# Encoder trunk on one Trainium2 core: output-projection operands, early gate/up units and GpSimd's share in attention

## The chip, the cores and the metric

The kernel runs on one core of a Trainium2 chip. The metric is the device time of one execution in microseconds (us). The core has five instruction streams that matter here: TensorE (PE in the profile, with PEld for the loading of weights), VectorE (DVE), ScalarE (ACT), GpSimd (POOL) and SyncE (SP), which only issues transfers. SP and POOL each have a queue of transfers; an instruction that waits holds up whatever stands behind it on its engine.

## The reference

Two layers over 512 tokens of 1024 channels, 16 heads of 64. Layer 0 mixes tokens by 2-D neighbourhood attention over an 8 x 64 grid, layer 1 by three dilated sliding windows with a distance penalty. Every layer is

```python
h = rms_norm(x, norm_mix_pre[layer])
h = neighbourhood_attention(h, ...) if layer % 2 == 0 else dilated_attention(h, ...)   # each ends in  o @ w_o
x = x + rms_norm(h, norm_mix_post[layer])
h = rms_norm(x, norm_ffn_pre[layer])
x = x + rms_norm(swiglu(h, w_gate, w_up, w_down), norm_ffn_post[layer])
```

with `swiglu(x) = (silu(x @ w_gate) * (x @ w_up)) @ w_down`. In layer 1 the scores of a window get `- slope[head] * distance` before the softmax, and -1e30 outside the window.

## The kernel before

**Arithmetic.** Every large product is made in three matmuls (`mm3`, L375 to L379): each operand is split into a high and a low part (`split`, L363: a copy with rounding on ScalarE, L364, a subtraction on VectorE, L365), and high x high, high x low and low x high are added in a PSUM bank. The query/key, value, gate/up and down products are also arranged as seven products of half-size blocks in place of eight. For gate/up and query/key a class `Seven` (L404) holds one *unit*, a pair of 128-column weight blocks over 512 tokens. Its first step, `first` (`p1` and `p2`), splits the raw weights and makes two products of 12 matmuls each, from the operands X1A and X1B (token tiles 0 and 1). The other steps need sums of weight blocks (`sums`, L441 to L451, adds on GpSimd and VectorE) and operands that also hold token tiles 2 and 3 (D1, S2, S4, S3, X2B). `run` (L551) orders the steps of a unit among those of the following ones.

**Stages.** Norm and transposes; values and then, head pair by head pair (j = 0 to 7), query/key unit and attention; output projection; gate/up, 22 units; down; then the same for layer 1.

**Neighbourhood attention** (L1115 to L1140): for each head, scores, `softmax` numerators in four blocks (`window_softmax`), one reciprocal for the row sums (L1132), a scaling of the four blocks by it on GpSimd (L1134), transposes, products with the values. `keep` (L1027) copies the result of a head pair out of PSUM, split in high and low, and sends it to DRAM (`rvd`) from GpSimd's queue; in layer 0 the copy puts the elements in another order, and it is the writing that is strided (L1139). The pair 7 stays on the chip.

**Dilated attention** (L1237 to L1271): the bias of a head is `SLOPES[head] * dist`, made on GpSimd (`bias`, L1239) from a table of distances in `memc`, in one buffer of 768 columns for both heads; `softmax_pair` subtracts it on VectorE (L1234).

**Output projection** (`mix_out`, L1036, and `out_proj`, L771): `rvd` is loaded back into `rxa`. Eight weight units k, 128 rows each, are split: four into the ring of split weights `wslot` (four buffers, L369, shared with the query/key and gate/up units), one into `rxa`, three into `rxb`. `product(t)` adds the eight k of one token tile in two banks, in the order of k. For each token tile follow the norm after the mixer (`post`), the norm before gate/up (`pre`) and the operands of gate/up (`ops`): `postnorm_sum` (L642), `prenorm` (L589, L591), additions on GpSimd (L622 to L628), transposes (L598) and their copies (L600, L601).

**Gate/up** (`gate_up`, L818): three units are begun before the loop over the 22; `sink` evacuates into `memc` (L834, L835). Raw weights lie in two buffers of a pool and in three of an arena that takes the place of `rxb`. `down` follows; its norm gain is loaded by `gain` (L573), from GpSimd's queue like the others.

**Memory.** `arena` (L332) stacks buffers on a left and a right side. In layer 0, attention's `ao0` and `akl` lie on the right; `memc` takes their place.

**Order.** The program's order is not the order of execution. `Order` (L130) takes all instructions, the dependences between them (also those through buffers of a ring, arenas that lie over one another, and banks) and a table of costs (`_cost`, L77), runs a list schedule forward and backward several times, and pins every engine's stream, SP's and POOL's too, to the order of the best run (`pin`, L279). So an edit of a few lines can move instructions anywhere.

Of the kernel before, what the change touches and what calls it, by code (L numbers as in the profile page):

```python
# [295 lines left out]
def encoder_kernel(ctx: ExitStack, tc: tile.TileContext, a: dict, out: bass.AP):  # L296
# [29 lines left out]
    mem = cpool.tile([P, MEM], F32, name="mem")  # L326
    rvd = [dpool.tile([PAIRS, P, D], F32R, name=f"rvd{i}") for i in range(2)]

# [243 lines left out]

    def gain(g, row, queue=nc.gpsimd):  # L573
        queue.dma_start(g, bass.AP(tensor=row.tensor, offset=row.offset, ap=[[0, P], [1, D]]))  # L574
        return g
# [242 lines left out]
    def gate_up(layer, xs, hid, more, rings, sums):  # L818
# [29 lines left out]

        ahead = 3
        for f in range(ahead):  # L850
            unit_of(f).first()
        for f in range(FT):
            for i in range(f, min(f + 2, FT)):
                if i not in us:
                    us[i], units[i].p5 = next(u_), next(p5_)
            run(unit_of(f), unit_of(f + 1), unit_of(f + ahead))
            if sums and f % 2 == 0:
                sums.pop(0)(units[f].added)
# [151 lines left out]
    def hl(mem, i, n):  # L1010
        return mem[:, i * D:i * D + n], mem[:, i * D + n:i * D + 2 * n]
# [15 lines left out]
    def keep(layer, j, o, ost_, view):  # L1027

        mem = next(ost_) if j < PAIRS - 1 else rxa[:, j * D:(j + 1) * D]
        h, l = (view(v) for v in hl(mem, 0, 512))  # L1030
        act.activation(h, o, AF.Copy)
        dve.tensor_sub(l, o, h.bitcast(F32))
        if j < PAIRS - 1:
            nc.gpsimd.dma_start(rvd[layer][j], mem)

    def mix_out(layer, w, rxb, load_x):  # L1036
        for j in range(PAIRS - 1):
            nc.gpsimd.dma_start(rxa[:, j * D:(j + 1) * D], rvd[layer][j])
        us = [None] * 4 + [hl(rxa, 8, D)] + [hl(rxb, 2 * i, D) for i in range(3)]

        out_proj(w, rv, layer, load_x, us, (ring(mem, 4 * D, D, 4), ring(mem, 0, D, 4), ring(mem, 13440, 512, 2)),
                 (mem[:, 11392:11392 + D], mem[:, 12416:12416 + D]))

    def ffn(layer, stack):
        hl_ = ring(rxc, 0, D, 5)
# [4 lines left out]
        with arena(f"raw{layer}", 6 * D) as more:  # L1050
            gate_up(layer, xs, hid, more, (ring(memc, 0, 512, 4), ring(memc, 2 * D, 512, 2), ring(mem, MEM - 512, 256, 2)),
                    sums[layer])
# [62 lines left out]
    for j in range(PAIRS):  # L1115
# [8 lines left out]
        for hd in range(2):  # L1124
            h = 2 * j + hd
            bt = next(bias_)
            nc.sync.dma_start(bt, a["na_bias"][h])
            mn, sm, rc = (small(f"{n}0_{h}", 4) for n in ("mn", "sm", "rc"))
            pr = (next(p_), next(p_))

            views = window_softmax(q, kd, kl, hd, bt, pr, mn, sm, f"0_{h}")
            dve.reciprocal(rc, sm)  # L1132
            for i in range(4):
                pool.tensor_scalar(views[i], views[i], rc[:, i:i + 1], 1.0, op0=ALU.mult, op1=ALU.mult)  # L1134
            pts.append(window_transposed(next(pt_), views, f"0_{h}"))
        o = bank("o", f"o0_{j}")
        window_pv(o, vq[j // 2], pts, j)

        keep(0, j, o.rearrange("p (c i) -> p c i", i=ROWS), ost_,  # L1139
             lambda v: v.rearrange("p (i c) -> p c i", i=ROWS))  # L1140

    inner.close()
    memc = ctx.enter_context(arena("memc", 3 * D, "right"))
    mix_out(0, a["na_o"], rxb, lambda xt, t: nc.sync.dma_start(xt, a["x_rows"][t]))
    stack.close()
    rxb = ffn(0, stack)


# [6 lines left out]
    pt_, few_ = ring(ap, 10 * D, D, 4), ring(mem, 0, 96, 2)  # L1155
    bt, dist, qs, ks = memc[:, 0:768], memc[:, 768:1536], memc[:, 1536:2048], memc[:, 2048:2560]
    p5_ = ring(memc, 2560, 256, 2)
    q_, k_, kl_, ost_ = rxc[:, 0:D], rxc[:, D:2 * D], rxc[:, 2 * D:3 * D], ring(rxc, 3 * D, D, 1)
    w22_ = w22_ring(rxc[:, 4 * D:5 * D])
    b6 = bt.rearrange("p (k c) -> p k c", c=P)  # L1160

    b2h = b6[:, 4:6], b6[:, 0:2]
    nc.gpsimd.dma_start(dist, a["dist"])

    def by_token(v):
# [70 lines left out]

    def bias(j, hd, c, o=None):  # L1237
        o = bt[:, c] if o is None else o
        pool.tensor_scalar(o, dist[:, c], SLOPES[2 * j + hd], 1.0, op0=ALU.mult, op1=ALU.mult)  # L1239

    def scores_a(j, hd, b2):
        if b2 == 0:
            bias(j, hd, slice(0, 4 * P))
        s, pr = bank("s", f"sa_{j}_{hd}_{b2}"), next(p_)
        for b in (2 * b2, 2 * b2 + 1):
# [6 lines left out]
            i0 = i if b % 2 == 0 else after(i, i0)  # L1252
        softmax_pair(pr, s, ((b6[:, 1:3], b6[:, 0:2]), (b6[:, 0:2], b6[:, 0:4:3]))[b2], stats[j][0], hd, b2)
        parts[0, j, hd, b2] = pr

    def scores_b(j, c2):

        if c2 == 0:
            bias(j, 0, slice(4 * P, 6 * P))
            bias(j, 1, slice(4 * P, 6 * P), bt[:, 0:2 * P])  # L1260
        ss = [bank("s", f"sb_{j}_{hd}_{c2}") for hd in range(2)]
# [253 lines left out]
```

## Time and profile before

| | |
|---|---|
| median of 3 runs | 1505.38 us (1505.06 to 1508.24) |
| profiled execution, own time | 1505.72 us |
| its span, first to last instruction | 1503.9 us |
| mean granted TensorE clock | 0.992 |
| DMA moved | 247.25 MB |

A line of the profile names an engine, a line of the kernel, an operation, `out<-in` by the names of buffers, and a duration; `[1.62 <-DVE ao L1032]` is idle time before an instruction and what ended it. A line "A:B" is a window in us from the start of the span. Matmuls overlap, so a busy TensorE counts each from its start to its modelled end. "PEclk" is the share of its full clock that TensorE was granted.

### The profile page before, as it was taken

Reading aid. Unit: us, or ns where it says so; the run is one execution under the profiler, and the core shown is the slowest. Engines: PE = TensorE matmul, PEld = TensorE weight load, DVE = VectorE, ACT = ScalarE, POOL = GpSimd, SP = SyncE. Lnnn points to the kernel's source line nnn. Section 1 sums busy time; section 2 is a strip of 40 time slices with the busy share of each in tenths; the row PEclk is TensorE's granted clock in tenths of the full one; section 3 lists DMA queues with packets and bytes.
Section 4 is the critical chain, followed back from the end, with each engine's and each line's share of the span. In section 5 each row is a group of like instructions: output and inputs, shape, how many; then the busy total and the mean of one; then the engine's idle time right before and its main releaser. Section 6 shows DMA issues by size and latency. Waiting matters only on the chain.

```text
span 1503.9 us, 27938 instructions
## 1 busy us (share of the span) xinstructions
PE 1450.8 (96%) x10788; PEld 1335.8 (89%) x10788; DVE 1206.0 (80%) x1884; ACT 895.1 (60%) x1787; POOL 604.8 (40%) x484
## 2 busy tenths in 40 slices
PE   7999999999999999999999999999998999999997
PEld 7988877899999888999999998888977999999885
DVE  5499976898998878788678667887748989898876
ACT  4477754555555657554467766877764645555664
POOL 5357754534331002676455554445316423330001
PEclk9999999999999999999999999999999999999999
DMA  5347483856474674455344875672664232234662
GB/s 197 134 177 173 159 288 139 244 155 194 154 190 146 188 227 160 138 156 189 119 141 161 191 210 162 191 167 89 218 205 168 85 113 101 97 105 148 202 206 88
DMA packets 82117, 247.25 MB, mean 164 GB/s; under 512 B 18816, under 2 KB 29056, under 8 KB 79936
## 3 DMA queue, kind: packets, MB, share of 16 engines
q1 hardware_dynamic: 70064, 180.32, 36.5%
q0 software_dynamic: 11776, 64.88, 16.3%
q8 instruction: 85, 1.39, 0.4%
q14 instruction: 48, 0.39, 0.1%
q10 hardware_dynamic: 144, 0.26, 0.0%
HBM read 223.31 MB, written 68.26 MB: 194 GB/s over the span
## 4 chain that ended last, share of the span: by engine, by line
PE 78%; DVE 9%; DMA 5%; ACT 4%; issue 2%; POOL 1%; SPq 0%; POOLq 0%; DVEq 0%; ACTq 0%
PE gu L376 9%; PE gu L377 9%; PE gu L378 9%; PE pp_d L376 4%; PE pp_d L378 4%; PE pp_d L377 4%; PE yd_s L376 3%; PE yd_s L377 3%; PE yd_s L378 3%; PE vd L376 2%; PE vd L377 2%; PE yd_pp L376 2%; PE vd L378 2%; PE yd_pp L377 2%; PE yd_pp L378 2%
## 5 line engine op out<-in xcount | busy, mean ns | idle before, releaser
L377 PE MATMUL gu<-rxa,h_b 128*128 128x256 f32 x352 | 99.4, 283 | 3.6 <-DVE rxa L601 3.6
L376 PE MATMUL gu<-rxc,h_a 128*128 128x256 f32 x352 | 100.0, 286 | 2.3 <-ACT rxc L600 2.3
L376 PE MATMUL gu<-rxa,h_b 128*128 128x256 f32 x352 | 98.9, 282 | 2.3 <-ACT rxa L600 2.3
L376 PE MATMUL gu<-rxa,h_c 128*128 128x256 f32 x352 | 99.9, 284 | 0.6 <-DVE memc L838 0.5
L377 PE MATMUL gu<-rxc,h_a 128*128 128x256 f32 x352 | 100.3, 285 | 0.0
L378 PE MATMUL gu<-rxc,l_a 128*128 128x256 f32 x352 | 100.2, 285 | 0.0
L378 PE MATMUL gu<-rxa,l_b 128*128 128x256 f32 x352 | 99.0, 282 | 0.0
L377 PE MATMUL gu<-rxa,h_c 128*128 128x256 f32 x352 | 98.5, 280 | 0.0
L378 PE MATMUL gu<-rxa,l_c 128*128 128x256 f32 x352 | 98.3, 280 | 0.0
L364 ACT ACTIVATE rxc<-mem 128x512 fp32r<-128x512 f32 (+2 forms) x90 | 55.8, 624 | 65.6 <-PE yd_pp L377 34.6
L444 POOL TENSOR_TENSOR raw<-raw 128x512 f32<-128x512 f32 x24 | 36.4, 1516 | 123.6 <-DVE l_a L365 109.4
L365 DVE TENSOR_TENSOR rxc<-mem,rxc 128x512 fp32r<-128x512 f32 (+2 forms) x90 | 65.6, 733 | 20.5 <-ACT rxc L364 18.7
L444 POOL TENSOR_TENSOR r_gu<-r_gu 128x512 f32<-128x512 f32 x20 | 29.9, 1495 | 109.1 <-DVE l_a L365 105.5
L444 POOL TENSOR_TENSOR r_d<-r_d 128x512 f32<-128x512 f32 x24 | 37.1, 1546 | 88.4 <-DVE l_ad L365 53.2
L377 PEld LDWEIGHTS gu<-rxa,h_b 128*128 128x128 f32 x352 | 67.0, 190 | 4.0 <-DVE rxa L601 4.0
L376 PEld LDWEIGHTS gu<-rxc,h_a 128*128 128x128 f32 x352 | 68.0, 194 | 2.8 <-ACT rxc L600 2.8
L1235 ACT ACTIVATE mem<-mem 128x256 f32<-128x256 f32 x128 | 63.6, 501 | 10.1 <-DVE mem L1234 9.8
L376 PEld LDWEIGHTS gu<-rxa,h_b 128*128 128x128 f32 x352 | 67.1, 191 | 2.7 <-ACT rxa L600 2.7
L376 PEld LDWEIGHTS gu<-rxa,h_c 128*128 128x128 f32 x352 | 66.3, 188 | 2.4 <-DVE memc L838 1.3
L377 PEld LDWEIGHTS gu<-rxc,h_a 128*128 128x128 f32 x352 | 68.0, 193 | 0.0
L378 PEld LDWEIGHTS gu<-rxc,l_a 128*128 128x128 f32 x352 | 67.6, 192 | 0.0
L574 POOL DMA_DIRECT2D mem<-g_ffn_post x2 | 1.2, 612 | 164.0 <-DVE rxc L365 164.0
(603 smaller groups left out, 6242.8 us busy)
## 6 DMA issues: line engine op xcount, KB each, us to landing
wsum<-wd POOLq DMA_DIRECT2D x24, 1408.0 KB, 11.4
r_d<-dil_qk SPq DMA_DIRECT2D x48, 512.0 KB, 4.8
raw<-wg SPq DMA_DIRECT2D x24, 512.0 KB, 3.7
raw<-wu SPq DMA_DIRECT2D x24, 512.0 KB, 4.7
wsum<-wsum POOLq DMA_DIRECT2D x8, 1408.0 KB, 8.0
raw<-wsum SPq DMA_DIRECT2D x22, 512.0 KB, 4.3
r_gu<-wg SPq DMA_DIRECT2D x20, 512.0 KB, 3.8
r_gu<-wu SPq DMA_DIRECT2D x20, 512.0 KB, 4.6
```

The lines of the kernel that those rows point to most:

```text
L364: act.activation(h, src, AF.Copy)
L365: dve.tensor_sub(l, src, h.bitcast(F32))
L376: i = pe.matmul(o, s[0], m[0], start=start, stop=False, skip_group_check=True)
L377: pe.matmul(o, s[0], m[1], start=False, stop=False, skip_group_check=True)
L378: pe.matmul(o, s[1], m[0], start=False, stop=stop, skip_group_check=True)
L444: self.added = e[0].tensor_add(q[0], q[0], q[2])
L574: queue.dma_start(g, bass.AP(tensor=row.tensor, offset=row.offset, ap=[[0, P], [1, D]]))
L1235: act.activation(pr[:, f], pr[:, f], AF.Exp, bias=st[:, c:c + 1], scale=-1.0, accum_out=st[:, c + 2:c + 3])
```

## The change

- `rvd` is an F32 buffer, and `keep` stores to it from SP's queue; loading it back stays with GpSimd's. `gain` uses SP's queue by default.
- Layer 0: the scalings of blocks 1 and 3 of each head go to ScalarE; blocks 0 and 2 stay on GpSimd. `keep` gets a view of the PSUM bank in the order of the output, so that its reading is strided and its writing contiguous.
- Layer 1: the bias of every head is computed on the host (`dil_bias`, 6 x 128 columns a head) and loaded in two pieces a head (four and two blocks) from SP's queue, into a buffer of 1536 columns, where each head and each kind of window has a place of its own. The table of distances and its load go.
- Output projection: units 2 and 3 are split into a new arena `wm` (3 x 1024 columns, the last half of unit 3 in `vmem`), not into the ring; the ring holds only units 0 and 1. `wm` is open only during the output projection; `memc` is opened anew after it, in each layer, in the same place.
- Gate/up: five units are begun before the loop, and the loop begins the sixth when it comes to f = 2. The ring of gate buffers has five, for that; the second buffer for `up` moves to `mem`.

```diff
-    rvd = [dpool.tile([PAIRS, P, D], F32R, name=f"rvd{i}") for i in range(2)]
+    rvd = [dpool.tile([PAIRS, P, D], F32, name=f"rvd{i}") for i in range(2)]
...
-    def gain(g, row, queue=nc.gpsimd):
+    def gain(g, row, queue=nc.sync):
...
-        ahead = 3
-        for f in range(ahead):
+        ahead, early = 3, 5
+        for f in range(early):
             unit_of(f).first()
...
-            run(unit_of(f), unit_of(f + 1), unit_of(f + ahead))
+            run(unit_of(f), unit_of(f + 1), unit_of(f + ahead) if f + ahead >= early else None)
...
-            nc.gpsimd.dma_start(rvd[layer][j], mem)
+            nc.sync.dma_start(rvd[layer][j], mem.bitcast(F32))
...
-    def mix_out(layer, w, rxb, load_x):
+    def mix_out(layer, w, rxb, wm, load_x):
...
-        us = [None] * 4 + [hl(rxa, 8, D)] + [hl(rxb, 2 * i, D) for i in range(3)]
+        us = [None] * 2 + [hl(wm, 0, D), (wm[:, 2 * D:], vmem), hl(rxa, 8, D)] + [hl(rxb, 2 * i, D) for i in range(3)]
...
-            gate_up(layer, xs, hid, more, (ring(memc, 0, 512, 4), ring(memc, 2 * D, 512, 2), ring(mem, MEM - 512, 256, 2)),
+            gate_up(layer, xs, hid, more, (ring(memc, 0, 512, 5), cycle([memc[:, 2560:3072], mem[:, 13520:14032]]), ring(mem, MEM - 512, 256, 2)),
...
-                pool.tensor_scalar(views[i], views[i], rc[:, i:i + 1], 1.0, op0=ALU.mult, op1=ALU.mult)
+                if i % 2:
+                    act.activation(views[i], views[i], AF.Copy, scale=rc[:, i:i + 1])
+                else:
+                    pool.tensor_scalar(views[i], views[i], rc[:, i:i + 1], 1.0, op0=ALU.mult, op1=ALU.mult)
...
-        keep(0, j, o.rearrange("p (c i) -> p c i", i=ROWS), ost_,
-             lambda v: v.rearrange("p (i c) -> p c i", i=ROWS))
+        keep(0, j, o.rearrange("p (c i) -> p i c", i=ROWS), ost_,
+             lambda v: v.rearrange("p (i c) -> p i c", i=ROWS))
...
-    memc = ctx.enter_context(arena("memc", 3 * D, "right"))
-    mix_out(0, a["na_o"], rxb, lambda xt, t: nc.sync.dma_start(xt, a["x_rows"][t]))
+    with arena("wm0", 3 * D, "right", F32R) as wm:
+        mix_out(0, a["na_o"], rxb, wm, lambda xt, t: nc.sync.dma_start(xt, a["x_rows"][t]))
     stack.close()
-    rxb = ffn(0, stack)
+    memc = inner.enter_context(arena("memc0", 3 * D, "right"))
+    rxb = ffn(0, stack, memc)
...
-    bt, dist, qs, ks = memc[:, 0:768], memc[:, 768:1536], memc[:, 1536:2048], memc[:, 2048:2560]
+    bt, qs, ks = memc[:, 0:1536].rearrange("p (k c) -> p k c", c=P), memc[:, 1536:2048], memc[:, 2048:2560]
...
-    nc.gpsimd.dma_start(dist, a["dist"])
...
-    def bias(j, hd, c, o=None):
-        o = bt[:, c] if o is None else o
-        pool.tensor_scalar(o, dist[:, c], SLOPES[2 * j + hd], 1.0, op0=ALU.mult, op1=ALU.mult)
+    def bias(j, hd, k, n):
+        v = bt[:, 6 * hd + k:6 * hd + k + n]
+        nc.sync.dma_start(v, a["dil_bias"][2 * j + hd, :, k:k + n])
...
-            bias(j, hd, slice(0, 4 * P))
+            bias(j, hd, 0, 4)
...
-            bias(j, 0, slice(4 * P, 6 * P))
-            bias(j, 1, slice(4 * P, 6 * P), bt[:, 0:2 * P])
+            for hd in range(2):
+                bias(j, hd, 4, 2)
...
-        "dist": _dist(),
+        "dil_bias": (np.reshape(SLOPES, (HEADS, 1, 1)).astype(np.float32) * _dist()).reshape(HEADS, P, 6, P),
```

More of the change, by code (lines that the diff above doesn't have):

```diff
@@ L1033, in keep, with ffn @@
         if j < PAIRS - 1:
-            nc.gpsimd.dma_start(rvd[layer][j], mem)
-    def mix_out(layer, w, rxb, load_x):
+            nc.sync.dma_start(rvd[layer][j], mem.bitcast(F32))
+    def mix_out(layer, w, rxb, wm, load_x):
         for j in range(PAIRS - 1):
             nc.gpsimd.dma_start(rxa[:, j * D:(j + 1) * D], rvd[layer][j])
-        us = [None] * 4 + [hl(rxa, 8, D)] + [hl(rxb, 2 * i, D) for i in range(3)]
+        us = [None] * 2 + [hl(wm, 0, D), (wm[:, 2 * D:], vmem), hl(rxa, 8, D)] + [hl(rxb, 2 * i, D) for i in range(3)]
         out_proj(w, rv, layer, load_x, us, (ring(mem, 4 * D, D, 4), ring(mem, 0, D, 4), ring(mem, 13440, 512, 2)),
                  (mem[:, 11392:11392 + D], mem[:, 12416:12416 + D]))
-    def ffn(layer, stack):
+    def ffn(layer, stack, memc):
         hl_ = ring(rxc, 0, D, 5)
@@ L1159, in encoder_kernel @@
     w22_ = w22_ring(rxc[:, 4 * D:5 * D])
-    b6 = bt.rearrange("p (k c) -> p k c", c=P)
-    b2h = b6[:, 4:6], b6[:, 0:2]
-    nc.gpsimd.dma_start(dist, a["dist"])
     def by_token(v):
@@ L1252, in scores_a @@
             i0 = i if b % 2 == 0 else after(i, i0)
-        softmax_pair(pr, s, ((b6[:, 1:3], b6[:, 0:2]), (b6[:, 0:2], b6[:, 0:4:3]))[b2], stats[j][0], hd, b2)
+        b4 = bt[:, 6 * hd:6 * hd + 4]
+        softmax_pair(pr, s, ((b4[:, 1:3], b4[:, 0:2]), (b4[:, 0:2], b4[:, 0:4:3]))[b2], stats[j][0], hd, b2)
         parts[0, j, hd, b2] = pr
@@ L1269, in scores_b @@
             pr = next(p_)
-            softmax_pair(pr, ss[hd], (b2h[hd], b2h[hd]), stats[j][1], hd, c2)
+            softmax_pair(pr, ss[hd], (bt[:, 6 * hd + 4:6 * hd + 6],) * 2, stats[j][1], hd, c2)
             parts[1, j, hd, c2] = pr
@@ L1423, in encoder_kernel @@
     inner.close()
-    mix_out(1, a["dil_o"], rxb, load_block)
+    with arena("wm1", 3 * D, "right", F32R) as wm:
+        mix_out(1, a["dil_o"], rxb, wm, load_block)
     stack.close()
-    ffn(1, stack)
+    memc = inner.enter_context(arena("memc1", 3 * D, "right"))
+    ffn(1, stack, memc)
+    inner.close()
     places = [(n, lo if side == "left" else ARENA - hi, hi if side == "left" else ARENA - lo, o, c)
```

## The prediction

> **What bounds the kernel now.** I read the page first, then a table of stages (busy time by window), then finer windows where TensorE is not full, then the timeline and the rows of the lines that the change touches.
>
> ```profile
> span 1503.9 us, 27938 instructions
> PE 1450.8 (96%) x10788; PEld 1335.8 (89%) x10788; DVE 1206.0 (80%) x1884; ACT 895.1 (60%) x1787; POOL 604.8 (40%) x484
> ```
>
> TensorE is idle for only 1503.9 - 1450.8 = 53.1 us. The change adds and removes no matmul, so it can win only idle time or time at a reduced clock. The windows (length, then busy time and count of PE, PEld, DVE, ACT, POOL, then granted clock, DMA share, GB/s) say where:
>
> ```profile
> 60.00:200.00 140.00, 133.55 (x1034) 119.38 (x1035) 126.65 (x277) 98.36 (x224) 89.85 (x101) 1.00 0.58 178
> 200.00:225.00 25.00, 23.27 (x123) 17.50 (x120) 16.56 (x44) 13.82 (x35) 14.03 (x22) 1.00 0.88 286
> 225.00:256.00 31.00, 31.00 (x147) 24.55 (x146) 18.28 (x24) 11.79 (x24) 8.46 (x9) 1.00 0.31 112
> 256.00:300.00 44.00, 37.07 (x284) 35.49 (x283) 39.45 (x50) 24.13 (x44) 28.33 (x21) 0.92 0.87 253
> 720.00:1100.00 380.00, 372.31 (x3115) 341.02 (x3114) 285.46 (x610) 271.07 (x683) 186.55 (x155) 1.00 0.58 168
> 1100.00:1150.00 50.00, 49.50 (x265) 40.09 (x265) 25.40 (x47) 24.04 (x57) 10.84 (x12) 1.00 0.47 151
> 1150.00:1180.00 30.00, 23.74 (x173) 22.28 (x172) 27.17 (x34) 17.95 (x31) 24.19 (x17) 0.89 0.41 145
> ```
>
> Idle TensorE: neighbourhood attention 6.45 us, its tail 1.73, the seam between output projection and gate/up 6.93 in layer 0 and 6.26 in layer 1, dilated attention 7.69. The other half of the 53 us (start, end, layer boundary) is untouched by the diff. Inside the seams:
>
> ```profile
> 257.00:262.00 5.00, 1.77 (x13) 1.12 (x11) 4.71 (x7) 3.00 (x7) 5.00 (x6) 0.97 0.84 301
> 262.00:265.00 3.00, 2.89 (x13) 2.62 (x14) 3.00 (x4) 2.80 (x5) 2.91 (x3) 0.50 1.02 418
> 265.00:278.00 13.00, 13.00 (x113) 12.79 (x112) 12.62 (x17) 7.81 (x14) 9.33 (x7) 1.00 0.86 224
> 278.00:282.00 4.00, 0.53 (x3) 0.30 (x2) 4.00 (x6) 1.46 (x3) 4.00 (x3) 1.00 0.69 184
> 282.00:285.00 3.00, 2.88 (x13) 2.89 (x14) 1.99 (x3) 0.35 (x1) 1.71 (x2) 0.52 1.05 305
> 1152.00:1156.00 4.00, 1.25 (x8) 0.84 (x8) 4.00 (x5) 2.19 (x4) 3.92 (x4) 1.00 0.98 342
> 1156.00:1163.00 7.00, 5.99 (x28) 5.92 (x29) 6.76 (x8) 3.08 (x6) 6.92 (x5) 0.52 0.90 327
> 1174.00:1178.00 4.00, 1.71 (x13) 1.33 (x12) 4.00 (x5) 3.04 (x6) 1.64 (x2) 1.00 0.07 8
> ```
>
> Each seam has two gaps. In layer 0, gap 1 (257 to 265) loses 3.23 + 0.11 us idle and 0.50 x 2.89 = 1.4 us to a halved clock, 4.8 in all; gap 2 (278 to 285) loses 3.47 + 0.12 + 0.48 x 2.88 = 5.0. In layer 1, gap 1 loses 2.75 + 1.01 + 0.48 x 5.99 = 6.6, gap 2 loses 2.29. Together 18.7 us: that is the main prize. VectorE is full in all four gaps (4.71 of 5.00, 4.00 of 4.00) and GpSimd in three.
>
> **The change part by part: the seams.** TensorE waits there for norms of the last token tiles and can run only the first two products (24 matmuls) of units of gate/up. 113 matmuls in 13.00 us is 0.115 us each, 2.8 us a unit.
>
> ```profile
> 255.00:277.80 22.80, 13.64 (x96) 12.50 (x96) 1.01 (x3) 1.11 (x3) 0.93 0.81 248
> 246.93 1.06 ACT L364 ACTIVATE h_a<-r_gu 128x1024 fp32r<-128x1024 f32 x1 [0.69 <-PE yo L378]
> 250.31 2.21 POOL L444 TENSOR_TENSOR r_gu<-r_gu 128x512 f32<-128x512 f32 x1 [2.56 <-DVE l_a L365]
> 258.17 1.26 POOL L445 TENSOR_TENSOR r_gu<-r_gu 128x512 f32<-128x512 f32 x1
> 245.11 1.28 DVE L591 SCALAR_TENSOR_TENSOR mem<-mem,rs_o 128x1024 f32<-128x1024 f32 x1 [0.66 <-POOL rs_o L584]
> 253.06 2.32 DVE L591 SCALAR_TENSOR_TENSOR mem<-mem,rs_o 128x1024 f32<-128x1024 f32 x1 [1.63 <-POOL rs_o L584]
> ```
>
> The first row (matmuls on the tile gu) has 96 = 4 x 24 matmuls before gap 2: four units are already begun in practice, so early = 5 adds one unit, 2.8 us, ahead of gap 2. In layer 0 that leaves 3.6 - 2.8 = 0.8 us idle; a gap that short should not halve the clock (the 2.29 us at 1174 left it at 1.00), so 2.8 + 1.4 = 4.2 come back. [...] In layer 1 gap 2 closes: 2.3. Bounds: 0 (the unit's split lands on the full VectorE and shifts the gap) to 5.0 and 2.3.
>
> Gap 1 comes from late operands. The first gate/up split waits for a split-weight buffer that the projection holds until 246.93, and the adds of the first two units, rows 250.31 to 258.17, then run on GpSimd in the seam, where the same L591 that took 1.28 us takes 2.32. With two projection operands outside the ring, two buffers are free before the weights are there, and these splits and adds can run once the loads land, by my estimate from about 231 (the tail, below: store landed about 221, two splits, one more load of some 5 us), up to 245, where DVE and POOL are slack (18.28 and 8.46 of 31.00). Against this stand the fifth unit's split and the split into vmem, which projection unit 3 now holds: both stay in the seam, so VectorE's load there hardly falls. The transposes still pass through two banks. I take a third of gap 1: 1.6 + 2.2 = 3.8 (bounds 0 and 11.4). Seams: 4.2 + 2.3 + 3.8 = **10.3 us won**.
>
> **Attention, layer 0.** The rows are min/median/max in ns:
>
> ```profile
> L1134 POOL TENSOR_SCALAR mem<-mem,rc x64: 361/476/2053, 96.2 to 223.3; 128x256 f32<-128x256 f32 x48, 128x128 f32<-128x128 f32 x16
> L1315 ACT ACTIVATE mem<-mem x128: 491/499/526, 804.8 to 1123.0; 128x256 f32<-128x256 f32 x128
> L1031 ACT ACTIVATE ao<-o x7: 1057/1077/1118, 129.0 to 216.2; 128x512 fp32r<-128x512 f32 x7
> L1031 ACT ACTIVATE rxc<-o x7: 574/592/600, 836.7 to 1098.0; 128x512 fp32r<-128x512 f32 x7
> L1032 DVE TENSOR_TENSOR ao<-o,ao x7: 1022/1050/1102, 132.2 to 217.2; 128x512 fp32r<-128x512 f32 x7
> L1032 DVE TENSOR_TENSOR rxc<-o,rxc x7: 632/683/690, 838.1 to 1098.6; 128x512 fp32r<-128x512 f32 x7
> L675 ACT ACTIVATE mem<-pp_d x16: 364/383/387, 744.7 to 1057.7; 128x256 f32<-128x256 f32 x16
> L675 ACT ACTIVATE mem<-pp_n x8: 368/384/385, 64.1 to 175.2; 128x256 f32<-128x256 f32 x8
> ```
>
> 32 of the 64 scalings go from GpSimd (0.476 us, 15.2 in all) to ScalarE (0.499 as in L1315, 16.0). keep writes contiguously and reads PSUM in strides of 8: as in layer 1 it should take 0.592 and 0.683 instead of 1.077 and 1.050, saving 8 x 0.485 = 3.9 us of ScalarE and 8 x 0.367 = 2.9 of VectorE. ScalarE gains 12.1 us of work where it has 140.00 - 98.36 = 41.6 free, which covers it; without that cover the 12.1 would show. A strided PSUM read is in the trace: L675 reads pp_d in strides of 4 and pp_n contiguously, 383 against 384 ns. [...] Freed VectorE and GpSimd time can win back at most the 6.45 us idle before 200; I take half, **3 us won** (bounds 0 and 6.45).
>
> **The tail of that attention.** The new buffer wm lies where ao0 and akl lay, so projection units 2 and 3 can be split only after the last store from ao0. Each bank takes its eight k in order, so every product stops after k = 1.
>
> ```profile
> 218.56 0.58 POOL L1034 DMA_DIRECT2D rvd<-ao  x1 [1.62 <-DVE ao L1032]
> rvd<-ao POOLq DMA_DIRECT2D x7, 512.0 KB, 5.3
> spill<-mem SPq DMA_DIRECT2D x12, 512.0 KB, 2.7
> 200.00:225.00 25.00, 14.93 (x58) 10.58 (x59) 0.00 (x0) 0.00 (x0) 1.00 0.88 286
> ```
>
> That store leaves at 218.56 and lands 5.3 us later; from SP, 2.7. Behind the wait stand, on ScalarE, whatever the planner puts after these splits, and on SP the loads of projection units 6 and 7 (their raw buffer holds 2 and 3 until then), of the residual rows and of gate/up. Until about 225 TensorE now fills with 58 projection matmuls (last row, tile yo). With k = 0 and 1 of two products only 24 remain: (58 - 24) / 58 x 14.93 = 8.8 us lost at most, 0 at least (attention there is quicker by its shorter scaling chain and has fewer splits ahead of it). I take **3 us lost**, nearer the lower end, since keep of pair 6 should come about 5 us sooner. In layer 1 wm lies over the bias buffers, whose last read in the trace is this:
>
> ```profile
> 1101.38 0.42 DVE L1234 CUSTOM_DVE_ANT_1 mem<-sa,memc 128x256 f32<-128x256 f32 x1
> ```
>
> Two splits after it (1.06 us each on ScalarE, as h_a above, and about as much behind them on VectorE) end near 1105, and 24 matmuls of k = 0 and 1, 24 / 58 x 14.93 = 6.2 us, cover that: nothing lost, or half of them, 12 matmuls or 3.1 us, if the cover is used up before.
>
> **Dilated attention and queues.**
>
> ```profile
> POOL memc L1239 <- DVE mem L1234: 54.0, 21, 6.1
> POOL rvd L1034 <- DVE rxc L1032: 19.2, 3, 15.9
> POOL mem L574 <- DVE rxc L365: 190.1, 3, 82.1
> mem<-na_bias SPq DMA_DIRECT2D x16, 192.0 KB, 2.4
> ```
>
> 32 GpSimd scalings become 32 loads from SP (6.3 MB more over 380 us, 17 GB/s beside 168). GpSimd no longer stands 54.0 us behind softmax with the units' adds queued after it. PE's 7.69 us idle bounds the gain; I take **2 us** (-2 to 7.7, as 14 stores and 7 norm gains move to SP too, where a wait like the 15.9 us of L1034, or part of the 82.1 us of g_ffn_post, would stand ahead of weight loads. The raw buffers loaded ahead hide a few us of it; nothing in the trace shows how much, and I count 0, up to 4 lost.)
>
> **Sum.** -10.3 - 3 + 3 - 2 = -12.3 us. The profiled execution took 1505.7 us (1503.9 span plus 1.8 around it), 0.3 above the median of 1505.38. Forecast 1493.4.
>
> **Rivals.** *Port-bound seams*: VectorE and GpSimd full in the gaps (4.00 of 4.00 both at 278) set the end, and one more unit changes nothing, since the planner began a fourth by itself: the change would not do there what it says. Only -3 + 3 - 2 = -2 is left: 1503.7. Against it: GpSimd's adds do get an earlier place. *Lost filler*, the slower side: the tail costs the whole 8.8 and 12 matmuls (3.1) in layer 1, attention and dilated win 1 each, and the seams only the fifth unit, 2 x 2.8: +8.8 + 3.1 - 2 - 5.6 = +4.3, 1510.0. It decides once the first matmul on a wm operand starts after about 230. *All closes*: seams -16, attention -4 without tail loss, dilated -2: -22, 1483.7; for it speaks that splits and adds of two units leave the full stretch.
>
> **How the numbers follow.** A measurement of this kernel can tell 0.2% (3.0 us) from no change: 1502.4 to 1508.4 is "same". Chances: forecast 0.52, all closes 0.17, port-bound 0.16, lost filler 0.15. Faster is the first two and 0.03 of port-bound, 0.72; same 0.13 of it and 0.02 of lost filler, 0.15; slower 0.13. The forecast's own range is 1487 to 1500; to 1484 and 1508 it takes in port-bound and half of all closes.
>
> **What would show it.** Right: 120 gu matmuls ahead of the first d1; no halved clock in gap 2; keep rows near 0.6 and 0.68; the first split of r_gu before 245. Wrong: gaps of the same length with VectorE full; TensorE idle for over 5 us between 195 and 225; SP waiting ahead of weight loads.

## The result and the profile after

| | before | after |
|---|---|---|
| median, runs side by side | 1505.95 us (1505.06 to 1508.24) | 1516.78 us (1513.56 to 1520.17) |
| profiled execution, span | 1505.72, 1503.9 us | 1517.70, 1515.9 us |
| mean granted clock | 0.992 | 0.988 |

The ratio is 1.0065, with a 95% interval of 1.004 to 1.009: 0.65% slower, where 1493.4 us was forecast. The head of the page of the kernel after:

```profile
span 1515.9 us, 27958 instructions
PE 1453.8 (96%) x10788; PEld 1338.2 (88%) x10788; DVE 1184.2 (78%) x1884; ACT 908.3 (60%) x1819; POOL 540.3 (36%) x398
```

GpSimd has the 64 us less that were meant (604.8 to 540.3), and VectorE 22 less. TensorE is idle for 62.1 us instead of 53.1. To see where, I took for both kernels the end of the last matmul on a stage's own tiles from the timeline; the stage lasts from the end before it (us):

| stage ends with the last matmul of | before: end, length | after: end, length | difference |
|---|---|---|---|
| projections of neighbourhood attention (pp_n) | 198.6, 198.6 | 193.1, 193.1 | -5.5 |
| its values (o) | 232.9, 34.3 | 221.6, 28.5 | -5.8 |
| output projection 0 (yo) | 256.5, 23.6 | 258.8, 37.2 | +13.6 |
| gate/up 0 (gu) | 495.8, 239.2 | 490.7, 231.9 | -7.3 |
| down 0 (yd) | 600.5, 104.8 | 593.3, 102.6 | -2.2 |
| values of layer 1 (vd) | 739.9, 139.3 | 734.5, 141.2 | +1.9 |
| query/key of dilated attention (pp_d) | 1090.0, 350.1 | 1108.8, 374.3 | **+24.2** |
| its values (o) | 1130.0, 40.0 | 1147.1, 38.3 | -1.7 |
| output projection 1 | 1150.9, 20.9 | 1171.1, 24.0 | +3.1 |
| gate/up 1 | 1390.0, 239.1 | 1403.7, 232.6 | -6.5 |
| down 1 | 1494.1, 104.1 | 1507.7, 104.1 | 0.0 |

The two gate/up stages, whose starts are the seams, won 13.8 us. Layer 0's attention and projection together changed by 2.3. The dilated stage, from the last vd to the last pp_d, lost 24.2 us, twice the whole difference. The windows of after that answer to those of before (busy time and count of PE, PEld, DVE, ACT, POOL, granted clock, DMA share, GB/s):

```profile
60.00:200.00 140.00, 137.10 (x1048) 120.95 (x1048) 124.35 (x288) 110.60 (x260) 71.47 (x73) 1.00 0.59 184
256.00:300.00 44.00, 41.67 (x338) 39.37 (x337) 36.11 (x52) 29.06 (x50) 28.22 (x20) 1.00 0.72 224
720.00:1100.00 380.00, 352.17 (x2922) 327.14 (x2921) 259.77 (x569) 253.71 (x634) 157.39 (x113) 0.97 0.58 169
```

In 256 to 300 TensorE is idle for 2.3 us instead of 6.9, with 338 matmuls instead of 284 and the clock at 1.00 instead of 0.92. In 720 to 1100 it is idle for 27.8 us instead of 7.7, and the clock is down to 0.97. The dilated stage in its own bounds, before and then after:

```profile
739.90:1090.00 350.10, 342.48 (x2865) 313.85 (x2863) 267.92 (x578) 254.92 (x642) 173.77 (x142) 1.00 0.59 169
```

```profile
734.50:1108.80 374.30, 346.69 (x2870) 320.89 (x2868) 258.35 (x578) 255.37 (x641) 149.31 (x109) 0.97 0.60 174
```

Idle time grew by 27.6 - 7.6 = 20.0 us, and the same matmuls (2870 records for 2865) took 346.7 - 342.5 = 4.2 us more, at the lower clock: that is the 24.2. VectorE and GpSimd have less work there than before, ScalarE the same, and the DMA share is the same. So something is waited for. Waits of VectorE, and the chain around the longest of them in the timeline (VectorE, then TensorE, then windows):

```profile
DVE mem L1215 <- DMA mem<-sw: 24.9, 5, 10.2
```

```profile
888.86 0.17 DVE L1215 TENSOR_TENSOR mem<-mem 128x8 f32<-128x8 f32 x1 [10.17 <-DMA mem<-sw]
...
890.36 0.60 DVE L685 TENSOR_TENSOR mem<-memc,pp_d 128x256 f32<-128x256 f32 x1
```

```profile
891.01 0.58 PE L376 MATMUL pp_d<-rxa,h_cd 128*128 128x256 f32 x1 [5.81 <-DVE mem L685]
```

```profile
885.20:891.00 5.80, 0.01 (x1) 0.00 (x0) 2.10 (x6) 1.16 (x2) 0.00 (x0) 0.80 0.99 279
891.00:894.00 3.00, 2.98 (x13) 2.76 (x13) 2.95 (x11) 0.02 (x1) 1.01 (x1) 0.50 0.00 1
956.60:961.40 4.80, 0.01 (x1) 0.03 (x1) 0.99 (x5) 0.13 (x1) 0.00 (x0) 0.89 0.64 175
961.40:965.00 3.60, 3.60 (x17) 3.60 (x18) 3.33 (x9) 3.26 (x7) 0.00 (x0) 0.50 0.00 0
```

L1215 is the first use of the *exchange*. Dilated attention adds two softmax parts whose statistics (minimum and sum of a row) lie on different partitions; 8 kB of them go to memory (`sw`, L1197) and come back in another order by four loads (L1199), and the weights worked out from them (L1215 to L1224) go the same way once more. VectorE stood for 10.17 us before L1215. The eviction L685 stands behind L1215 in VectorE's stream, TensorE's next product stands behind that eviction, and so TensorE was empty for 5.81 us; then it ran at half its clock (0.50 in 891 to 894). The wait that ended last on TensorE names L685, an eviction of 0.60 us: TensorE's own waits do not show the exchange, VectorE's do. (The chain on the page of the kernel after lists `DMA mem<-sw` with 3% of the span, where that of the kernel before has no such entry; but old_bias, a quick kernel below, has 4%, so the entry alone does not show a loss.) The same happens at 956.6: L1215 starts at 960.36 after a wait of 6.96 us, and TensorE, empty for 4.80 us, is shown to wait for a memset (L434) behind it.

What the exchange met there, by SP's stream in the timeline and by the transfers of the window 872 to 889 (KB each, median us from issue to landing):

```profile
877.02 0.33 SPq L360 DMA_DIRECT2D r_d<-dil_qk  x1
877.66 1.75 SPq L1199 DMA_DIRECT2D mem<-sw  x4
879.50 0.38 SPq L1305 DMA_DIRECT2D mem<-vd  x1
879.93 0.50 SPq L360 DMA_DIRECT2D r_d<-dil_qk  x1
```

```profile
wsum<-wd POOLq DMA_DIRECT2D x1, 1408.0 KB, 11.2
r_d<-dil_qk SPq DMA_DIRECT2D x2, 512.0 KB, 7.6
mem<-vd SPq DMA_DIRECT2D x1, 512.0 KB, 10.9
...
mem<-sw SPq DMA_DIRECT2D x4, 2.0 KB, 6.7
```

Beside it, in the waits of SP, stood the new bias loads, which wait until softmax has freed their buffer, and hold up what is behind them on SP:

```profile
SPq L1240 <- DVE mem L1234: 85.7, 15, 13.8
```

### The profile page after: what moved, and what is told of

It is laid out like the page before. It is cut to its first block, busy times and chain, and to the rows that moved or that the text cites. A ratio compares the mean times of both kernels' runs of the same rounds, so it can differ in the third digit from the quotient of the medians.

```text
span 1515.9 us, 27958 instructions
## 1 busy us (share of the span) xinstructions
PE 1453.8 (96%) x10788; PEld 1338.2 (88%) x10788; DVE 1184.2 (78%) x1884; ACT 908.3 (60%) x1819; POOL 540.3 (36%) x398
## 4 chain that ended last, share of the span: by engine, by line
PE 72%; DVE 9%; ACT 7%; DMA 6%; issue 2%; POOL 2%; SPq 1%; POOLq 0%; DVEq 0%; ACTq 0%
PE gu L376 9%; PE gu L377 9%; PE gu L378 9%; PE pp_d L376 3%; PE pp_d L378 3%; PE pp_d L377 3%; DMA mem<-sw 3%; PE yd_s L376 3%; PE yd_s L378 3%; PE yd_s L377 3%; PE yd_pp L376 2%; PE yd_pp L378 2%; PE yd_pp L377 2%; PE yo L376 2%; PE yo L377 2%
## 5 line engine op out<-in xcount | busy, mean ns | idle before, releaser
L584 POOL TENSOR_TENSOR rs_yd<-v_yd,mhalf 128x1 f32<-128x1 f32 x8 | 8.3, 1042 | 264.1 <-DVE v_yd L582 264.1
L456 ACT ACTIVATE mem<-gu 128x256 f32<-128x256 f32 x44 | 16.8, 383 | 90.1 <-PE gu L378 90.1
L376 PEld LDWEIGHTS gu<-rxa,h_b 128*128 128x128 f32 x352 | 66.5, 189 | 0.8 <-ACT h_b L364 0.6
L378 PEld LDWEIGHTS gu<-rxa,l_b 128*128 128x128 f32 x352 | 66.3, 188 | 0.9 <-DVE l_b L365 0.9
```

Of the source, the lines that this page charges most:

```text
L376: i = pe.matmul(o, s[0], m[0], start=start, stop=False, skip_group_check=True)
L378: pe.matmul(o, s[1], m[0], start=False, stop=stop, skip_group_check=True)
L456: act.activation(self.p5, self.right, AF.Copy)
L584: pool.tensor_tensor(r, v, mhalf, op=ALU.pow)
```

## The experiments

Ratios are to runs of the kernel before beside each; brackets are 95% intervals. "Stage" is the dilated stage as in the table above.

### First theory: bias loads that wait on SP hold up the exchange

**old_bias** puts the bias back on GpSimd and keeps all else of the change.

```diff
...
-        nc.sync.dma_start(v, a["dil_bias"][2 * j + hd, :, k:k + n])
+        pool.tensor_scalar(o, dist[:, c], SLOPES[2 * j + hd], 1.0, op0=ALU.mult, op1=ALU.mult)
...
```

> The changed kernel with the bias of dilated attention made on GpSimd again, as before; all else changed. The changed kernel's dilated attention (end of the value units to the last query/key matmul) took 374.3 us against 350.1. If the bias loads are the cause, by whatever way (queue or traffic), that stretch comes back to 345 to 353 us and the whole to 1488 to 1496 us, faster than the kernel before by the 13.8 us that the two gate/up stages won. If the stores of the attention results on SP's queue are the cause, the stretch stays at 370 or more and the whole above 1512. If it is chance in the new order of the planner, anything between 345 and 380 may come.

Measured: 1490.82 us, ratio 0.9891 [0.9866, 0.9917], stage 351.3, and gate/up kept its gain (232.2 and 232.6).

**only_bias** is the kernel before with the bias loads alone, the same edit the other way round.

> The kernel before with nothing but the bias loads added (and GpSimd's scalings of the distances gone). If the loads by themselves cost the 24 us, dilated attention takes 370 to 378 us and the whole 1525 to 1532. If they cost only together with the stores and norm gains on the same queue, it takes 350 to 358 us and the whole 1505 to 1513. If the change had been right in what it meant, GpSimd freed, it would be 348 and 1503.

Measured: 1511.6 us, ratio 1.0026 [1.0007, 1.0045], stage 362.1, between the two ranges that were given for it. VectorE and ScalarE waited 4.4 and 4.9 us for the exchange there, and no gap of TensorE is over 2.6 us.

**bias_pool_queue** issues the same loads from GpSimd's queue.

```diff
-        nc.sync.dma_start(v, a["dil_bias"][2 * j + hd, :, k:k + n])
+        nc.gpsimd.dma_start(v, a["dil_bias"][2 * j + hd, :, k:k + n])
```

> The changed kernel with the bias loads issued from GpSimd's queue instead of SP's: the same bytes, the same buffers, another queue. If waiting at the head of SP's queue is the cause (SP stood 85.7 us before bias loads until softmax had freed their buffer), dilated attention comes back to 345 to 358 us and the whole to 1490 to 1503. If the 6.3 MB more of traffic are the cause, it stays at 368 to 378 and the whole above 1510.

Measured: 1495.54 us (two executions), ratio 0.9914 [0.989, 0.9937], stage 353.5. The 6.3 MB alone do not cost the time: they still move.

**landing4** tells the planner that every transfer lands after 4 us.

```diff
-SYNC, RATE, LANDING, AHEAD = 50.0, 350.0, 2000.0, 1000.0
+SYNC, RATE, LANDING, AHEAD = 50.0, 350.0, 4000.0, 1000.0
```

> The changed kernel, its planner told that a transfer lands after 4 us and not after 2; the program is the same, only the order of each engine's stream differs. If VectorE's stands for the swapped statistics (24.9 us, 8.3 before) come of an order built on too early a landing, they fall under 10 us and dilated attention to 350 to 360 us, the whole to 1494 to 1505. If SP's queue itself is the bound, waits move but the stretch stays above 365.

Measured: 1518.38 us (two executions), ratio 1.0065 [1.0042, 1.0088]; no wait for the exchange in the stage, which still took 359.0, and gate/up 0 at 244.0 and gate/up 1 at 237.4: the seams' gain went. (The 8.3 us "before" in the expectation are of the whole kernel; in the stage VectorE waited 4.6.)

old_bias and bias_pool_queue spoke for the theory; only_bias lost half of what it should have, and landing4 got rid of the waits without getting back to 350. And each of the four is planned anew, so each also has another order.

### The parts, and other queues

**store_pool** gives the attention outputs' stores back to GpSimd's queue; **sw_pool** gives it the exchange.

```diff
-            nc.sync.dma_start(rvd[layer][j], mem.bitcast(F32))
+            nc.gpsimd.dma_start(rvd[layer][j], mem.bitcast(F32))
...
-        nc.sync.dma_start(d[:, :4 * n], in_)
+        nc.gpsimd.dma_start(d[:, :4 * n], in_)
...
```

(The four loads of the exchange move with its store.)

> The changed kernel with the attention outputs' stores issued on GpSimd's queue again (in both layers); the bias loads stay on SP. The dilated stage took 374.3 us in the changed kernel, 362.1 in the kernel before with only the bias loads added, 351.3 in the changed kernel without them. Theory (the waiting bias loads on SP do more harm where other issues stand on SP behind and around them, the stores among them): about half of the difference between 374.3 and 362.1 or more goes, the stage takes 360 to 368 us and the time is 1502 to 1511 us. Rival (the stores have no part; the order that the planner happens to write makes the difference): the stage stays within 4 us of 374 and the time within 3 us of 1516.8.

> The changed kernel with the swapped statistics' store and loads (10 DMAs for each pair of heads) issued on GpSimd's queue; the bias loads stay on SP, with their waits. Theory (the loss comes mainly by the statistics that stand behind a waiting bias load: VectorE waited 24.9 us for them): VectorE's waits at L1215 fall to under 10 us, the dilated stage falls from 374.3 to 352 to 360 us, the time is 1494 to 1503 us. Rival (the loss comes mainly by the weight loads that stand behind it): VectorE's waits at L1215 go all the same, but the stage stays above 366 us and the time above 1509 us.

Measured: store_pool 1491.82 us, 0.9898 [0.9875, 0.992], stage 350.7, better than its theory allowed. sw_pool 1492.23, 0.99 [0.9871, 0.9929], stage 345.5, the shortest of all and below the theory's 352 to 360, though what follows shows that it is no proof of it. In sw_pool the bias loads wait on SP longer than in the changed kernel, and nothing is lost:

```profile
SPq L1240 <- DVE mem L1234: 93.3, 17, 16.5
```

**seam_only** is the kernel before with `wm`, `early` and the gate buffers; **light_only** is it with GpSimd's lighter work and SP's stores and gains, without the bias loads.

> The kernel before with only the operands of the projection outside the ring and the five units begun early. Theory (the seams' gain is these edits alone, and the projection's longer time of layer 0 in the changed kernel, 37.2 us for 23.6, comes of its starting earlier): the two gate and up stages take 231 to 234 us each for 239.2 and 239.1, the projection of layer 0 ends at 255 to 258 us, the time is 1491 to 1495 us. Rival (the new operands wait for the attention's buffers that they lie over, as the forecast counted with 3 us and at most 8.8): the gate and up stages gain the same, but the projection of layer 0 ends at 259 to 265 us and the time is 1496 to 1503 us.

> The kernel before with only the lighter GpSimd work: every other scaling of neighbourhood attention on ScalarE, keep's strides, the outputs' stores and the norm gains on SP; no bias loads, no early units, no new operands. Theory (the projection of layer 0 is held by something with a time of its own, and so gives back what attention gains): neighbourhood attention ends at 217 to 222 us for 232.9, the projection still ends at 251 to 256 us for 256.5, the time is 1502 to 1507 us. Rival (the new operands held the projection back in the changed kernel): attention ends as early, the projection takes its 23.6 us of before and ends at 241 to 246 us, the time is 1491 to 1497 us.

Measured: seam_only 1513.82 us, 1.0043 [1.0027, 1.0059]. Gate/up took 235.3 and 232.6, which is 10.4 us won, yet the stage took 362.4 and the time lies outside both ranges. light_only 1505.86, 0.9988 [0.9972, 1.0004]; its attention ended at 230.2 and output projection 0 at 251.5 (5.0 earlier than before, as the theory said of the projection, while attention ended later than either range), gate/up took 236.6 and 238.7, the stage 362.9. In seam_only attention ended at 220.9 and the projection took 37.5, ending at 258.4: so the -5.8 and +13.6 of the table are one shift between the two stages, not a quicker attention and a slower projection. It comes without any edit in attention, and it hangs on the order too: after_sync45 below, which has `wm`, took 40.4 and 22.0. Neither kernel has a bias load, seam_only has no edit at all in dilated attention, and both lost over 12 us there. In each the longest gap of TensorE (4.5 and 5.9 us) stands behind the exchange, this time its second leg, for which ScalarE waits; seam_only, then light_only:

```profile
951.23 1.71 ACT L1316 ACTIVATE mem<-mem 128x256 f32<-128x256 f32 x4 [5.63 <-DMA mem<-sw]
```

```profile
913.42 2.50 ACT L1320 ACTIVATE mem<-mem 128x256 f32<-128x256 f32 x6 [4.82 <-DMA mem<-sw]
```

So waiting bias loads are not needed for the loss, and are not enough for it.

### Second theory: the order

**after_sync60** and **before_sync60** change one cost in the planner; every instruction and queue stays.

```diff
-SYNC, RATE, LANDING, AHEAD = 50.0, 350.0, 2000.0, 1000.0
+SYNC, RATE, LANDING, AHEAD = 60.0, 350.0, 2000.0, 1000.0
```

> The changed kernel with one number of the planner changed, the cost that it counts for a hand-over between engines (60 ns for 50): every instruction and every queue is the same, only the order that the planner writes differs. Theory (the dilated stage's loss of 24 us is mostly the order that the planner happened to write, in which the swapped statistics land late at two or three places and TensorE empties): the stage falls from 374.3 to 345 to 363 us, VectorE's waits at L1215 from 24.9 us to under 12, the time to 1488 to 1506 us. Rival (the waiting bias loads on SP cost it by themselves, in any order): the stage stays within 5 us of 374, the time at 1512 to 1521 us.

> The kernel before with the same number of the planner changed and nothing else. Theory (the planner's order alone moves the dilated stage): the stage differs from 350.1 by 4 us or more to either side, and the time from 1507 by as much; the most likely side is slower, 1509 to 1520 us, since 350.1 is at the short end of what the other kernels of this study showed in it (345 to 374). Rival (the order is worth little): within 3 us of 350.1 and of 1507.

Measured: after_sync60 1497.87 us, 0.9934 [0.9913, 0.9954], stage 364.5 (its bound was 363) with 8.0 us of waits at L1215 and 10.8 of ScalarE for the second leg. before_sync60 1507.72, 0.9997 [0.9982, 1.0012], stage 356.8: 6.7 longer, made up elsewhere, so the time did not move as expected.

**seam_sw_pool** and **before_sw_pool** are seam_only and the kernel before with the exchange on GpSimd's queue.

> The kernel before with the projection's operands outside the ring and five units begun early (1513.8 us, its dilated stage 362.4), and the swapped statistics' store and loads on GpSimd's queue. Theory (a late landing of the statistics is what empties TensorE and halves its clock): no gap of TensorE over 3 us in the dilated stage, the granted clock there 1.00 for 0.97, the stage 345 to 354 us, the time 1494 to 1506 us. Rival (something else that the order brings makes the stage long): gaps over 3 us stay, the stage 358 us or more, the time 1509 us or more.

> The kernel before with only the swapped statistics' store and loads on GpSimd's queue. VectorE waits for them for 4.6 us in the kernel before and TensorE has no gap over 1.3 us in that stage, so the theory (late statistics are the cost) allows little here: the dilated stage 345 to 352 us for 350.1, the time 1499 to 1509 us. Rival (GpSimd's queue itself is the quicker place for all of the stage, or the other way round): the stage moves by over 6 us.

Measured: seam_sw_pool 1510.03 us, 1.0008 [0.9995, 1.0021]. Its stage is 350.4, the clock 1.00, no gap over 1.6 us, as expected, but the projection of layer 0 ended at 266.9 instead of 258.4, and the time stayed above the theory's range. before_sw_pool 1520.48, 1.0088 [1.0061, 1.0114], stage 355.7, both outside the theory's ranges: a loss, and spread over the stages. A queue as such is no cure.

**after_sync45** and **old_bias_sync60** are one more order of the kernels with and without the bias loads.

> The changed kernel in a third order of the planner (its hand-over cost 45 ns for 50, nothing else). Theory (the shipped order is an unlucky one, and most orders of the same instructions are better): the stage 346 to 368 us, the time 1488 to 1506 us. Rival (the bias loads on SP make every order but a lucky one slow): the stage over 368 us, the time over 1508 us.

> The changed kernel without its bias loads (1490.8 us, dilated stage 351.3) in a second order (hand-over cost 60 ns for 50). Theory (without the bias loads on SP the stage is short in most orders): within 6 us of 351, the time 1486 to 1498 us. Rival (351.3 was a lucky order, and the loads are not what sets the stage): over 360 us, the time over 1500 us.

Measured: after_sync45 1517.43 us, 1.0059 [1.0037, 1.0081], stage 370.8, the rival's. old_bias_sync60 **1483.61 us**, 0.984 [0.9802, 0.9879], stage 352.4: the fastest of this study. In after_sync45 the wait lies with ScalarE; from the waits of the dilated stage:

```profile
ACT mem L1317 <- DMA mem<-sw: 17.0, 3, 8.5
```

### The order held, one thing changed

To separate order and queue, **same_order_bias_pool** and **same_order_sw_pool** are planned as the changed kernel is, and only then is one sort of transfer issued by GpSimd: TensorE's, VectorE's and ScalarE's streams are the changed kernel's, instruction for instruction, and SP's and GpSimd's differ by what moved.

```diff
-            n, e = len(self.all), ENGINES.index(str(i.engine).split(".")[-1])
+            n, e = len(self.all), 4 if i.name in MOVED else ENGINES.index(str(i.engine).split(".")[-1])
...
-        nc.sync.dma_start(v, a["dil_bias"][2 * j + hd, :, k:k + n])
+        MOVED.add(nc.gpsimd.dma_start(v, a["dil_bias"][2 * j + hd, :, k:k + n]).ins.name)
```

> The changed kernel in its own order: the planner counts the bias loads as SP's, so TensorE, VectorE and ScalarE run exactly the changed kernel's order, and then the bias loads are issued on GpSimd's queue instead. Theory (issues that stand behind a waiting bias load on SP come late, and that is the loss): the dilated stage falls from 374.3 to 348 to 358 us, VectorE's waits at L1215 from 24.9 us to under 8, the time to 1488 to 1501 us. Rival (the order of the engines is itself bad, whatever SP does): the stage stays above 366 us, the time above 1508 us.

> The changed kernel in its own order, TensorE, VectorE and ScalarE unchanged, with only the swapped statistics' store and loads issued on GpSimd's queue; the bias loads still wait on SP ahead of weight loads and stores. Theory (late statistics are the larger part of the loss): VectorE's waits at L1215 under 8 us, the stage 350 to 362 us, the time 1490 to 1505 us. First rival (the weight loads behind the bias loads are the larger part): the waits at L1215 go, the stage stays at 364 to 372 us, the time at 1506 to 1514 us. Second rival (the order itself): no change, 1513 to 1520 us.

Measured: 1513.4 us, 1.0028 [1.0002, 1.0054], and 1516.74, 1.0048 [1.0018, 1.0078]. Both stages are as long as in the changed kernel; window of the stage and waits, the first kernel and then the second:

```profile
732.50:1108.10 375.60, 348.19 (x2870) 321.57 (x2868) 261.12 (x578) 255.11 (x641) 163.21 (x137) 0.96 0.60 173
```

```profile
DVE mem L1215 <- DMA mem<-sw: 25.3, 5, 9.5
```

```profile
731.20:1106.60 375.40, 348.99 (x2870) 322.12 (x2868) 257.05 (x578) 255.52 (x642) 182.58 (x179) 0.97 0.59 174
```

```profile
DVE mem L1215 <- DMA mem<-sw: 22.5, 6, 7.7
```

The first theory falls here. With no bias load on SP this order waits for the exchange as long as before; with the exchange on GpSimd's queue VectorE waits about as long and ScalarE longer (12.8 us for 4.1). The exchange takes longer than the order gives it, on either queue.

**no_exchange_wait** keeps every stream, SP's and GpSimd's too, and takes away only the waiting for the exchange: the softmax weights are worked out from the statistics as they stand, without the swapped ones, so it leaves out what the exchange is for.

```diff
-        dve.tensor_tensor(by2(mn), stat(ta, 0), stat(sb, 0), op=ALU.min)
+        planned(dve.tensor_tensor(by2(mn), stat(sa, 0), stat(sb, 0), op=ALU.min), stat(ta, 0), stat(sb, 0))
...
-        weight[j] = ga, w[:, 8:16]
+        weight[j] = w[:, 0:8], w[:, 8:16], ga, w[:, 8:16]
```

> The changed kernel with every engine and queue in exactly the changed kernel's order, but the weights of the two softmax parts are worked out from the statistics as they stand, without the swapped ones: the exchange's store and loads are still issued, and nothing waits for what they bring (so the weights are not the reference's). Theory (the loss in this order is the exchange's late landing): TensorE's gaps over 3 us in the dilated stage go, its granted clock there is 1.00 for 0.97, the stage takes 346 to 358 us for 374.3, the time is 1488 to 1501 us. Rival (the order is slow for other waits, those of the weight splits and evictions on VectorE, and the statistics only seem to be last): the stage stays above 364 us, the time above 1506 us.

Measured: 1491.61 us, 0.9916 [0.9892, 0.9939]. The stage, and SP's wait for the bias buffer, which is still there:

```profile
731.50:1084.20 352.70, 340.95 (x2870) 315.36 (x2868) 259.08 (x578) 254.69 (x642) 148.21 (x109) 0.99 0.64 185
```

```profile
SPq L1240 <- DVE mem L1234: 80.0, 15, 13.7
```

374.3 - 352.7 = 21.6 of the 24.2 us are gone, with the longest gap of TensorE 2.0 us, and the whole kernel is 1516.8 - 1491.6 = 25 us quicker. In this order the late exchange is nearly all of the loss.

**exchange_landing6** tells the planner the exchange's real time.

```diff
-                    end = pipe + LANDING
+                    end = pipe + (LANDING if size > 10000 else 6000.0)
```

> The changed kernel, bias loads on SP, with the planner told that a transfer under 10 kB (the exchange alone) lands 6 us after its place in the pipe instead of 2; all other transfers keep 2. Theory (the order was bad because the exchange was planned too short): VectorE and ScalarE wait under 8 us in all for the exchange, the dilated stage is 345 to 358 us, the gate and up stages keep 231 to 234, the time is 1484 to 1501 us. Rival (the planned landing is not it): the stage over 364 us, the time over 1506 us.

Measured: 1535.54 us, 1.0205 [1.0184, 1.0227], the slowest, and the rival's. The waits for the exchange nearly went from the stage:

```profile
DVE mem L1215 <- DMA mem<-sw: 2.6, 1, 2.6
```

But the stage took 364.9, and the attention left over after it 67.2 us where the changed kernel took 38.3, at a clock of 0.90, with another 7.3 us of ScalarE's waits for the exchange:

```profile
1100.50:1167.70 67.20, 53.59 (x320) 40.40 (x319) 30.25 (x73) 36.71 (x90) 7.29 (x8) 0.90 0.48 148
```

As I read it, the weighing and the values, planned later, pile up behind the last projections, where nothing fills TensorE; nothing was run to test that. A truer number in one place does not make the planner's order a good one.

## Why the prediction was wrong

- **Seams, 10.3 won: right, and somewhat small.** The two gate/up stages won 7.3 + 6.5 = 13.8. By 279.2 TensorE had begun 122 matmuls of gate/up (120 forecast); gap 2 of layer 0 is 0.36 us and the halved clock is gone. Gap 1 closed by more than the third that was taken: the first splits of `r_gu` start at 226.25 and 235.03 instead of 246.93, and GpSimd's adds at 228.65 instead of 250.31. seam_only alone won 10.4 there, light_only 3.0, which the forecast had not counted. Matmuls on gu up to gap 2, then the first split and the first add:

```profile
256.00:279.20 23.20, 16.23 (x122) 14.68 (x122) 1.79 (x5) 1.51 (x4) 1.00 0.57 205
```

```profile
226.25 1.06 ACT L364 ACTIVATE h_a<-r_gu 128x1024 fp32r<-128x1024 f32 x1 [0.21 <-DMA r_gu<-wg]
```

```profile
228.65 1.30 POOL L444 TENSOR_TENSOR r_gu<-r_gu 128x512 f32<-128x512 f32 x1 [12.41 <-DVE l_a L365]
```

- **Attention of layer 0, 3 won: right.** TensorE's idle time from 60 to 200 fell from 6.45 to 2.90 us, 3.55 won. `keep` takes what layer 1's rows said, 0.579 and 0.691 us for 0.592 and 0.683:

```profile
L1031 ACT ACTIVATE ao<-o x7: 576/579/602, 114.0 to 207.2; 128x512 fp32r<-128x512 f32 x7
```

```profile
L1032 DVE TENSOR_TENSOR ao<-o,ao x7: 685/691/692, 117.4 to 207.8; 128x512 fp32r<-128x512 f32 x7
```

- **Its tail, 3 lost: right within its bounds.** The first matmul on `wm` starts at 217.64, well before the 230 from which the slower rival decides, so that rival did not come about. Attention and projection together ended 2.3 us later than before in the profiled execution; three kernels with the same streams there (the two of the held order and no_exchange_wait) ended it at 256.1, 256.1 and 255.9, so 2 to 3 us of it belong to that execution, in which the clock was halved from 216.2 to 219.7 and in the three it was not. The even balance that the forecast gave is what these show, but not its two sizes: the last pp_n came 4.7 to 6.0 us earlier in the four executions, and from there to the end of the projection they took 4.3 to 7.8 us longer, so that by this cut both terms were taken too small and their agreement in sum is partly luck. TensorE was idle for only 1.8 us between 195 and 225. The first matmul on `wm`:

```profile
217.64 2.33 PE L376 MATMUL yo<-wm,rxa 128*128 128x512 f32 x5
```

- **Dilated attention and queues, 2 won: wrong, 24.2 lost.** This is the step that failed: "I take 2 us (-2 to 7.7 ...)". It costed the moved issues one by one, as waits on SP "ahead of weight loads". Such waits came (85.7 us at L1240), and they cost next to nothing in the held order. What it held fixed was the order. An edit lets the planner order the stage anew, and in the new order the exchange came back late: VectorE waited 4.6 us for it in the order before, 24.9 in the order after, and without the waiting 21.6 of the 24.2 us were gone (no_exchange_wait). The waits on `sw` were in the trace of before, short, with 14 exchanges in the stage and nothing to say how much slack they had. The range should have held the price of some of them coming late, by my estimate 5 to 6 us for a gap (5.81 and 4.80 in the rows) and 1 to 2 for the clock behind it (the 4.2 us more of TensorE's busy time, over these two gaps and a shorter one at 791.8).
- **The signs.** All four that the prediction named for being right came about (120 matmuls, no halved clock in gap 2, the `keep` rows, the first split before 245), and of those for being wrong only SP's waits. None of them looks at the exchange.
- **The clock.** In the two long gaps it fell from 1.00 to 0.50 at about 888.7 and 960.4, some 3.5 and 3.8 us after TensorE's last matmul, and after the gap of 0.36 us it did not. It came back to 1.00 only at 898.9 and 967.2, 7.9 and 5.8 us after the matmuls did:

```profile
885.20:888.60 3.40, 0.01 (x1) 0.00 (x0) 0.00 (x0) 0.00 (x0) 0.00 (x0) 1.00 1.04 224
888.70:891.00 2.30, 0.00 (x0) 0.00 (x0) 2.10 (x6) 1.16 (x2) 0.00 (x0) 0.50 0.93 359
894.00:898.90 4.90, 4.90 (x20) 4.12 (x21) 1.42 (x2) 3.61 (x10) 3.01 (x3) 0.50 0.47 135
899.00:902.00 3.00, 3.00 (x31) 2.75 (x30) 1.47 (x3) 1.60 (x3) 0.00 (x0) 1.00 0.96 298
```

The return took about as long in the row 1156 to 1163 of the kernel before, 0.52 over 7 us, where the clock was at 1.00 by 1163.0, 6.0 us after the matmuls at 1157.01. In gap 1 of layer 0 there it was back by 265.2, only 3.3 us after those at 261.89, so the traces give the return no one length. Nor was a long gap needed: the halving at 216.2 followed 3.4 us in which TensorE was busy for 1.74 us with no gap over 1.26, so the prediction's "a gap that short should not halve the clock" held in its place (1.00 after the 0.36 us) and did not hold at 216.2:

```profile
212.80:216.20 3.40, 1.74 (x8) 0.89 (x6) 1.35 (x1) 2.74 (x4) 2.30 (x3) 1.00 0.95 324
216.30:219.60 3.30, 3.30 (x10) 2.38 (x10) 1.76 (x2) 0.54 (x1) 0.00 (x0) 0.50 0.59 154
```

Taken without the exchange's lateness the kernel runs 1491.6 us, near the 1493.4 forecast. That is partly luck, since the seams won 3.5 us more than forecast; and no_exchange_wait has no exchange wait at all, so this only bounds what the parts are worth.

**What stays open.** That the late exchange is the loss is shown for the changed kernel's order alone. Elsewhere waits for it and the stage's length do not go together: old_bias_sync60 waited 12.2 us on VectorE and 4.0 on ScalarE in a stage of 352.4, only_bias 4.4 and 4.9 in one of 362.1, landing4 not at all in one of 359.0. What those two lost there was not tested. Open too is why the orders with bias loads fell out badly. The change as it is has 374.3, 364.5 and 370.8 in three orders, without its bias loads 351.3 and 352.4 in two. But with them and another queue for stores or exchange it has 350.7 and 345.5, and kernels without them reached 362.9. That bias loads on SP lead the planner to such orders may be so and is not shown; how they would was not tried.

## What to carry over

Where a planner or compiler orders the streams, an edit's effect is its own cost plus a new draw of the order: here the draw alone moved the changed kernel between 1497.9 and 1517.4 us, though it left the kernel before where it was (before_sync60). Time an edit in more than one order before crediting or blaming it, and to test a cause hold the streams and remove one wait. And look in the profile for round trips through memory in the middle of an engine's stream: here VectorE's short waits in the kernel before (4.6 us in all) did not say how much slack was left (24.9 in the kernel after), and where TensorE ran empty for 5.81 us behind VectorE's wait of 10.17, the loss showed under another name, L685, the eviction that stood behind.

## What the hardware showed unexpectedly

The exchange's loads could take as long as large transfers: four loads of 2 kB issued from 877.66 on took 3.0 to 9.8 us to land, 6.7 in the median, and let L1215 start only at 888.86, while one transfer of 1.4 MB (11.2 us to land) and three of 0.5 MB (7.6 in the median of two, and 10.9) were issued or under way. The DMA share from the first issue to that start:

```profile
877.66:888.86 11.20, 7.55 (x78) 6.99 (x74) 1.03 (x2) 2.96 (x7) 4.20 (x4) 0.99 0.95 201
```

2 us is what the planner counts for the landing of every transfer. In the changed kernel the 64 loads of the exchange, of 1 and 2 kB, took 1.6 us from issue to landing at the least, 3.8 in the median and 11.5 at most (1.5, 3.1 and 8.0 in the kernel before): only the quickest of them came within 2. Changing the issuing queue did not help in that order (22.5 us of VectorE's waits on GpSimd's queue, 24.9 on SP's).
